# Split weights in three buffers in the input projections, and the odd layer's queries, keys and values in passes over 512 columns

## The chip, the cores and the metric

The kernel runs on one core of a Trainium2 chip. The metric is the device time of one execution in microseconds, the median of several; the profile is one further execution, taken by the hardware profiler.

## What is computed

Two sequences, of 1024 and 2048 tokens with 1024 channels, go through two layers with shared weights. The even layer projects the normed input, feeds half of it to a bidirectional S5 mixer and half to a bidirectional RWKV-7 mixer, gates both and projects back. The odd layer is windowed attention:

```python
def odd_layer(x, p):
    h = rms_norm(x, p['norm'])
    o = attn_branch(h @ p['w_in'], p)
    return x + (o.astype(x.dtype) @ p['w_out']).astype(x.dtype)

q, k, v, z = jnp.split(h, [1024, 1280, 1536], axis=-1)        # of h @ w_in
q = rms_head(q, p['at_q_norm']) * 64 ** -0.5                  # 16 heads of 64
k = rms_head(k, p['at_k_norm'])                               # 4 heads of 64
```

The S5 branch keeps 64 complex states in each of 32 groups of 16 channels and adds a direct term with `s5_d`. The RWKV branch takes r, k and v (512 columns each) and two low-rank inputs (128 columns) from the same projection, shifted by one token to both sides.

## The kernel before

Four programs run one after the other: `input_u` with `s5_consts` (normalize, project u, store the normed tokens h and u), `input_rkv` with `s5` (project r, k, v and the low-rank inputs, beside the S5 mixer), the mixers (gates and RWKV), and `even_out`, `odd_in` and `attention` together. In the first, second and last, class `Program` records every instruction and puts them in an order of its own: `put` (lines 345 to 396) keeps a list for each engine, estimates costs, and sends each engine's instructions in that order. Therefore nearly all instructions carry line 412 in the trace and are told apart by tile and shape. Every tile of a program lies in a few arenas named `sb` and `ps`; a new program takes over the memory of the one before.

All large products are made in two parts: a float32 operand is split into a rounded `hi` and a rest `lo`, and each product is hi·hi + hi·lo + lo·hi, three matmuls per block of 128 rows, 24 per product (`product_T`, line 593; `project_rows`, line 1725).

`input_u` (line 651) stores u in four parts of 128 channels, each 1024 tokens in one store, and then writes zeros into the four columns that separate the two sequences (lines 673 to 677).

`input_rkv` (line 698) goes over six segments of 512 tokens. For each it loads the stored tokens (`stored_T`, eight loads through a tile `full` with three buffers, each split by ACT and DVE) and makes 13 products of 128 columns: the low-rank inputs first (block 12), then for p = 0 to 3 the blocks k, r, v (4+p, p, 8+p). `split_weight` (line 635) loads a block of weights and splits it in the first segment, stores it to `wsp`, and loads it from there, 1 MB, in the others. The tile `wboth` has two buffers (line 723): a weight can be loaded when the product before the last one is done.

`s5` (line 1583) makes 8 rounds of four groups. Each round computes `cw` on DVE (6 operations of 1152 columns), the inverse products `wi0`, `wi1` on DVE (6 operations of 1024 columns), the strip on PE (matmuls with 16 output rows), stores the strip and loads it back twice in another layout as `k0`, and transposes the inverse products on PE into `iw`. Then each group loads its u, makes products with `iw` (`px`) and, after a scan, with `k0` and `cw` (`py`).

`odd_in` (line 1824) goes over the same six segments; per segment it makes 6 passes over 256 columns of the weights for queries, keys and values (two token tiles share one PSUM bank), normalizes by heads on ACT, DVE and POOL (the power on POOL), and then 8 products of 128 columns for the gate z, whose moving operand is 512 tokens.

## Time and profile before

| | us |
|---|---|
| median of 3 runs | 4057.89 (4054.45 to 4062.0) |
| the profiled execution | 4065.39 |
| its span (first to last instruction) | 4063.7 |
| PE busy | 3763.6 (93%) |
| DVE busy | 2821.8 (69%) |
| ACT busy | 1939.8 (48%) |
| POOL busy | 1615.8 (40%) |
| mean granted clock of TensorE | 0.970 |

A busy PE is not a PE at its peak: matmuls overlap, and their ends are modelled. The count of matmuls in a stretch without gaps tells their rhythm better than their mean duration. A wait stands in brackets behind the instruction that ended it, with what released it. SPq is the queue from which all transfers are issued; a DMA share of 1.0 is 16 engines busy.

### The profile page before, as it was taken

Reading aid. Unit: us, or ns where it says so; the run is one execution under the profiler, and the core shown is the slowest. Engines: PE = TensorE matmul, PEld = TensorE weight load, DVE = VectorE, ACT = ScalarE, POOL = GpSimd, SP = SyncE. Lnnn points to the kernel's source line nnn. Section 1 sums busy time; section 2 is a strip of 40 time slices with the busy share of each in tenths; the row PEclk is TensorE's granted clock in tenths of the full one; section 3 lists DMA queues with packets and bytes.
Section 4 is the critical chain, followed back from the end, with each engine's and each line's share of the span. In section 5 each row is a group of like instructions: output and inputs, shape, how many; then the busy total and the mean of one; then the engine's idle time right before and its main releaser. Section 6 shows DMA issues by size and latency. Waiting matters only on the chain.

```text
span 4063.7 us, 87721 instructions
## 1 busy us (share of the span) xinstructions
PE 3763.6 (93%) x34128; PEld 3118.4 (77%) x34128; DVE 2821.8 (69%) x5545; ACT 1939.8 (48%) x4847; POOL 1615.8 (40%) x2007
## 2 busy tenths in 40 slices
PE   6878999999899999999998799999999999999999
PEld 4656766676688888878876577999999977778777
DVE  8356655666568878888887676544444469899997
ACT  3334333333345565555655322333323357777776
POOL 4422322232364555555540242222222335555554
PEclk9989999999999999999999899999999999999999
DMA  5677565566543334333344666644444422222221
GB/s 154 162 174 228 162 191 173 174 191 188 176 154 101 119 112 127 119 106 115 119 115 98 216 233 214 206 148 155 143 157 147 147 84 72 77 81 74 76 66 58
DMA packets 536324, 570.32 MB, mean 140 GB/s; under 512 B 93602, under 2 KB 436770, under 8 KB 525924
## 3 DMA queue, kind: packets, MB, share of 16 engines
q1 hardware_dynamic: 535908, 564.72, 45.4%
q8 instruction: 268, 4.39, 0.5%
q14 instruction: 148, 1.21, 0.1%
HBM read 398.03 MB, written 166.56 MB: 139 GB/s over the span
## 4 chain that ended last, share of the span: by engine, by line
PE 45%; DVE 17%; DMA 4%; issue 4%; POOL 3%; ACT 2%; SPq 1%; DVEq 0%; ACTq 0%; POOLq 0%
PE ps L412 30%; DVE sb L412 11%; PE acc L887 5%; PE pc L1333 2%; PE acc L970 2%; PE pg L1186 2%; ACT sb L412 2%; DMA rk<-rk 1%; DVE ng L1251 1%; DVE z L1253 1%; PE pY L1356 1%; PE pc L1320 1%; POOL lt L1165 1%; PE pc L1311 1%; DVE lt L1206 1%
## 5 line engine op out<-in xcount | busy, mean ns | idle before, releaser
L412 PE MATMUL ps<-sb 128*128 128x512 f32 (+8 forms) x12464 | 2542.2, 359 | 153.2 <-DVE sb L412 48.4
L412 PEld LDWEIGHTS ps<-sb 128*128 128x128 f32 (+2 forms) x12464 | 1958.8, 187 | 555.7 <-DVE sb L412 105.0
L412 POOL TENSOR_TENSOR sb<-sb,sb 128x384 f32<-128x384 f32 (+5 forms) x468 | 469.5, 1021 | 444.2 <-ACT sb L412 226.0
L412 POOL TENSOR_TENSOR sb<-sb 128x512 f32<-128x512 f32 (+5 forms) x358 | 320.7, 899 | 675.0 <-ACT sb L412 325.8
L412 DVE TENSOR_TENSOR sb<-ps,sb 128x512 fp32r<-128x512 f32 (+4 forms) x620 | 402.0, 661 | 189.7 <-PE ps L412 115.5
L412 POOL TENSOR_TENSOR sb<-sb,mhalf 128x8 f32<-128x8 f32 (+3 forms) x156 | 223.0, 1431 | 644.4 <-DVE sb L412 640.5
L887 PE MATMUL acc<-h,w 128*128 128x128 f32 x3072 | 448.0, 290 | 17.0 <-POOL rt L1280 14.3
L887 PEld LDWEIGHTS acc<-h,w 128*128 128x128 f32 x3072 | 383.1, 196 | 42.5 <-POOL rt L1280 14.5
L412 ACT ACTIVATE sb<-sb 128x256 fp32r<-128x256 f32 (+9 forms) x392 | 276.1, 710 | 286.3 <-DVE sb L412 128.5
L412 ACT COPY sb<-ps 128x512 f32<-128x512 f32 (+4 forms) x402 | 195.1, 502 | 438.0 <-PE ps L412 429.3
L412 PE MATMUL ps<-ident,sb 128*128 128x128 f32 x1888 | 317.2, 280 | 55.5 <-DVE sb L412 51.1
L412 DVE TENSOR_TENSOR sb<-sb,sb 128x256 fp32r<-128x256 f32 (+6 forms) x259 | 265.8, 1038 | 142.9 <-ACT sb L412 128.8
L412 ACT ACTIVATE sb<-sb,sb 128x384 f32<-128x384 f32 (+3 forms) x486 | 299.3, 619 | 111.5 <-DVE sb L412 60.4
L412 PEld LDWEIGHTS ps<-ident,sb 128*128 128x128 f32 x1888 | 237.6, 143 | 119.9 <-DVE sb L412 72.1
L1165 POOL TENSOR_TENSOR lt<-rk,lb 64x256 f32<-64x256 f32 x288 | 216.9, 761 | 196.3 <-PE pY L1356 84.8
L412 ACT ACTIVATE sb<-ps 128x512 f32<-128x512 f32 x108 | 64.5, 597 | 385.7 <-PE ps L412 385.7
L1325 ACT COPY rt<-pc 32x128 f32<-32x128 f32 x768 | 196.7, 256 | 97.7 <-PE pc L1320 86.6
L412 DVE CUSTOM_DVE_ANT_0 sb<-ps,sb,sb 128x384 f32<-128x384 f32 (+1 forms) x384 | 215.3, 588 | 28.6 <-PE ps L412 27.1
L1150 POOL TENSOR_TENSOR kb<-rk,f 128x128 f32<-128x128 f32 x384 | 197.6, 546 | 76.1 <-PE pg L1196 67.6
L412 ACT CAST sb<-ps 128x512 fp32r<-128x512 f32 x368 | 202.1, 587 | 50.9 <-PE ps L412 46.0
L1340 DVE TENSOR_TENSOR rt<-pc,wc 64x256 f32<-64x256 f32 x376 | 158.3, 421 | 71.5 <-PE pc L1334 36.1
L412 DVE TENSOR_SCALAR sb<-sb,sb 128x384 f32<-128x384 f32 (+4 forms) x264 | 190.6, 751 | 18.2 <-POOL sb L412 16.2
(121 smaller groups left out, 4680.1 us busy)
## 6 DMA issues: line engine op xcount, KB each, us to landing
sb<-wsp SPq DMA_DIRECT2D x65, 1024.0 KB
rk<-rk SPq DMA_DIRECT2D x96, 512.0 KB
sb<-in_od_w_in SPq DMA_DIRECT2D x36, 1024.0 KB
h<-h SPq DMA_DIRECT2D x48, 512.0 KB
sb<-in_od_w_z SPq DMA_DIRECT2D x24, 1024.0 KB
qkv<-sb SPq DMA_DIRECT2D x72, 256.0 KB
sb<-qkv SPq DMA_DIRECT2D x72, 256.0 KB
sb<-in_x_sample SPq DMA_DIRECT2D x32, 512.0 KB
```

What stands on the lines that cost most here:

```text
L412: self.ops.append((eng, self.cost(eng, op, outs[-1] if outs[-1] is not k.get("accum_out") else outs[0], ins, a, k), deps, self.rank, lambd ...
L887: nc.tensor.matmul(sums[n][1][:, m * P:m * P + P], w[:, k, m * P:m * P + P], acts[n][0][:, k], start=k == 0, stop=k == KT - 1)
L970: nc.tensor.matmul(ps[:, 256 * (m % 2):256 * (m % 2) + 256], uw_at(k)[:, m], act_at(n)[:, 2 * k:2 * k + 2], start=k == 0, stop=k == 3)
L1150: nc.gpsimd.tensor_tensor(kb[:, sl, :, x, :], arr[n][:, sl, cs], f1[:, sl, cs, a:a + 32], MULT)
L1165: (nc.gpsimd if eng == "POOL" else nc.vector).tensor_tensor(ltv[:, :, :, at:at + 32], arr[n][rows, :, cs], f2[rows, :, cs, off:off + 32], ...
L1186: nc.tensor.matmul(g[64:P, c1, p], kb[0:64, p, c1].rearrange("c s i -> c (s i)"), lt[0:64, c1, 4 + p, 0:64], start=True, stop=True)
L1206: nc.vector.tensor_tensor(lt[rows, :, us, 0:64], g[rows], self.tri[h["d"]][rows].unsqueeze(1).unsqueeze(1).broadcast_to([64, 2, 4, 64]), MULT)
L1251: nc.vector.tensor_tensor(tv, z[:, 0:k, k:k + 1].broadcast_to([P, k, 31 - k]), z[:, k:k + 1, k + 1:32].broadcast_to([P, k, 31 - k]), MULT)
L1253: nc.vector.tensor_tensor(z[:, 0:k, k + 1:32], z[:, 0:k, k + 1:32], tv, ADD)
L1325: nc.scalar.copy(rt[rows, c1, 2 * q:2 * q + 2, :], pu[rows, 2:4])
L1333: nc.tensor.matmul(pu[0:64, 4 + p, :], lt[:, c1, 4 + p, 64:P], rt[:, c1, 4 + p, :], start=True, stop=True)
L1340: nc.vector.tensor_tensor(nrt[rows, n4 % 2, 4 - 4 * o:8 - 4 * o, :], pu[rows, 4:8], nh["wc"][rows, :, n4:n4 + 1].broadcast_to([64, 4, 64]) ...
```

## The change

Four parts. `input_u` gives its output tiles four more columns, clears them on POOL for the last part of the first sequence, and stores them with u; the four stores of zeros go. In `input_rkv` the pools are opened first, the pool of the weights has three buffers, and block 12's weight and the tokens of a segment are asked for together by `lead`, for the first segment ahead of the column loads. In `s5` the strip, its store and the loads of `k0` come ahead of the inverse products; the strip and both inverse products share the one buffer of a tile `wi`. In `odd_in` the six passes over 256 columns become three over 512: `wide_weight` loads two halves into tiles of 512 columns with two buffers, one token tile fills one PSUM bank, and the last pass holds the keys (normalized) and the values (copied).

```diff
+    WW = 2
...
+    def wide_weight(self, w):
+        nc = self.nc
+        hi = self.wp.tile([P, KT, 512], F32R, name="whi512", bufs=self.WW)
+        lo = self.wp.tile([P, KT, 512], F32R, name="wlo512", bufs=self.WW)
+        for c in (0, 256):
+            raw = self.wp.tile([P, KT, 256], F32, name="wraw256", bufs=2)
+            nc.sync.dma_start(raw, w[:, c:c + 256].rearrange("(k p) c -> p k c", p=P))
+            nc.scalar.copy(hi[:, :, c:c + 256], raw)
+            nc.vector.tensor_tensor(lo[:, :, c:c + 256], raw, f32(hi[:, :, c:c + 256]), SUB)
+        return [[x[:, k, :] for k in range(KT)] for x in (hi, lo)]
...
-                us = [op.tile([P, 8, min(1024, max(self.L)) // 8], F32, name=f"u{p}")[:, :, :T // 8] for p in range(4)]
+                us = [op.tile([P, 8, min(1024, max(self.L)) // 8 + 4], F32, name=f"u{p}") for p in range(4)]
+                pad = 4 if s == 0 and t0 + T == L else 0
+                if pad:
+                    for x in us:
+                        nc.gpsimd.memset(x[:, :, T // 8:T // 8 + pad], 0.0)
...
-        zero = cp.tile([P, 8, 4], F32, name="zero")
-        nc.gpsimd.memset(zero, 0.0)
-        n0 = self.col[0] + self.L[0] // 8
-        for p in range(4):
-            nc.sync.dma_start(self.u[p].rearrange("g c j n -> (g c) j n")[:, :, n0:n0 + 4], zero)
...
-        self.wp = st.enter_context(tc.tile_pool(name="wp", bufs=2))
+        self.wp = st.enter_context(tc.tile_pool(name="wp", bufs=3))
+        lead = lambda s, t0: (self.split_weight(12, W[:, LW0:LW0 + P]), self.stored_T(self.sp[s]["h"], t0, min(self.seg, self.L[s] - t0)))
+        first = lead(0, 0)
...
-                h = self.stored_T(t["h"], t0, T)
+                (w12, h), first = first or lead(s, t0), None
...
-            wr = [wp.tile(shp, F32, name=f"wi{i}") for i in range(2)]
-            strip = wp.tile([16, NG, 31, 16], F32, name="strip")
+            strip = wp.tile([16, 2 * NG * 256], F32, name="wi")[:, :NG * 496].rearrange("c (g t i) -> c g t i", g=NG, i=16)
...
+            wi = wp.tile([P, 2, NG, 16, 16], F32, name="wi")
+            wr = [wi[:, i] for i in range(2)]
...
-                for c in range(6):
-                    wt = self.weight([W[:, 256 * c:256 * c + 256]])
-                    for i in range(0, nt, 2):
-                        ps = self.psm.tile([P, 2, 256], F32, name="acc")[:, :n]
+                for c in range(3):
+                    wt = self.wide_weight(W[:, 512 * c:512 * c + 512])
+                    for i in range(nt):
+                        ps = self.psm.tile([P, 512], F32, name="acc")
+                        self.project_rows(None, [(his[k][:, sl], los[k][:, sl]) for k in range(8)], wt, slice(0, 512), ps)
+                        n = 512 if c < 2 else 256
+                        if c == 2:
+                            nc.scalar.copy(o[:, n:], ps[:, n:])
...
+                        nc.sync.dma_start(t["qkv"][ti // 2][:, ti % 2, 512 * c:512 * c + 512], o)
```

The order that comes of it differs at three places that the prediction speaks of. The first is SP's queue where the second program begins; `u_0` to `u_3` are the stores of u and of the zeros, `in_rw_...` the column loads, `h0_0` the tokens of the first segment, `in_ev_w_in` a block of weights, `wsp12` the store of block 12. Before:

```order
L412 DMA u_3_228<-sb1_283 1024x1x128
L412 DMA u_2_227<-sb0_282 1024x1x4
L412 DMA u_3_228<-sb0_282 1024x1x4
L412 DMA sb0_1644<-in_rw_mu 128x13x1
L412 DMA sb0_1644<-in_rw_k_k 128x4x1
L412 DMA sb0_1644<-in_rw_k_a 128x4x1
L412 DMA sb0_1644<-in_rw_r_k 128x4x1
L412 DMA sb0_1644<-in_rw_a0 128x4x1
L412 DMA sb1_1645<-in_rw_a_up 64x512
L412 DMA sb1_1645<-h0_0_106 128x4x128 x3
L412 DMA sb1_1645<-in_ev_w_in 128x8x128
L412 DMA sb1_1645<-u_0_225 128x1x388 x2
```

With the change:

```order
L412 DMA u_3_228<-sb1_283 1024x1x128
L412 DMA sb1_1644<-in_ev_w_in 128x8x128
L412 DMA sb1_1644<-h0_0_106 128x4x128 x3
L412 DMA sb0_1643<-in_rw_mu 128x13x1
L412 DMA sb0_1643<-in_rw_k_k 128x4x1
L412 DMA sb0_1643<-in_rw_k_a 128x4x1
L412 DMA sb0_1643<-in_rw_r_k 128x4x1
L412 DMA sb0_1643<-in_rw_a0 128x4x1
L412 DMA sb1_1644<-in_rw_a_up 64x512
L412 DMA sb1_1644<-u_0_225 128x1x388 x2
L412 DMA wsp12_253<-sb2_1645 128x2048
L412 DMA sb1_1644<-h0_0_106 128x4x128 x3
```

The stores of 4 columns are gone, the weight and three token loads stand first, and the store of the split weight stands ahead of the next token loads.

The second is SP's queue at the fourth of the eight strips; `wsp9`, `wsp6` and `wsp2` are weights in the order in which PE uses them, `strip3` is the strip's store and its two loads. Before:

```order
L412 DMA bon1_144<-sb1_1645 64x384 x2
L412 DMA rk1_126<-sb1_1645 128x3x128
L412 DMA sb2_1646<-wsp9_250 128x2048
L412 DMA strip3_236<-sb1_1645 16x1984
L412 DMA sb1_1645<-strip3_236 128x4x256 x2
L412 DMA sb2_1646<-wsp6_247 128x2048
L412 DMA rk1_126<-sb1_1645 128x3x128 x2
L412 DMA sb2_1646<-wsp2_243 128x2048
L412 DMA rk1_126<-sb1_1645 128x3x128
```

With the change:

```order
L412 DMA bon1_144<-sb1_1644 64x384 x2
L412 DMA rk1_126<-sb1_1644 128x3x128
L412 DMA sb2_1645<-wsp6_247 128x2048
L412 DMA strip3_236<-sb1_1644 16x1984
L412 DMA sb1_1644<-strip3_236 128x4x256 x2
L412 DMA sb2_1645<-wsp2_243 128x2048
L412 DMA sb2_1645<-wsp10_251 128x2048
L412 DMA rk1_126<-sb1_1644 128x3x128 x2
L412 DMA bon1_144<-sb1_1644 64x384 x2
```

Weight 6 stood behind the strip's loads and stands ahead of the strip's store now; weight 2 is the first one behind them.

The third is PE at the same strip: the last strip products (16 rows) and what follows; `ps0` and `ps1` with 128x512 are the projections, `ps4` with 128x128 the transposes of the inverse products. Before:

```order
L412 MATMUL ps4_1654<-sb1_1645 16x256 x2
L412 MATMUL ps4_1654<-sb1_1645 16x16 x2
L412 MATMUL ps4_1654<-sb1_1645 16x240 x2
L412 MATMUL ps1_1651<-sb2_1646 128x512 x5
L412 MATMUL ps4_1654<-ident_60,sb1_1645 128x128 x4
L412 MATMUL ps1_1651<-sb2_1646 128x512
L412 MATMUL ps2_1652<-heads2_67,sb1_1645 128x2 x3
L412 MATMUL ps1_1651<-sb2_1646 128x512 x2
L412 MATMUL ps4_1654<-ident_60,sb1_1645 128x128
L412 MATMUL ps1_1651<-sb2_1646 128x512
L412 MATMUL ps4_1654<-ident_60,sb1_1645 128x128
```

With the change:

```order
L412 MATMUL ps4_1653<-sb1_1644 16x240
L412 MATMUL ps0_1649<-sb2_1645 128x512
L412 MATMUL ps4_1653<-sb1_1644 16x240
L412 MATMUL ps3_1652<-sb1_1644 128x384
L412 MATMUL ps1_1650<-sb2_1645 128x512 x14
L412 MATMUL ps2_1651<-heads2_67,sb1_1644 128x2 x3
L412 MATMUL ps1_1650<-sb2_1645 128x512 x10
L412 MATMUL ps0_1649<-sb2_1645 128x512 x4
L412 MATMUL ps3_1652<-ident_60,sb1_1644 128x128 x3
L412 MATMUL ps0_1649<-sb2_1645 128x512 x4
L412 MATMUL ps4_1653<-ident_60,sb1_1644 128x128 x2
L412 MATMUL ps0_1649<-sb2_1645 128x512 x16
```

Before, five projection matmuls stood between the last strip product and the transposes; now there are 32.

## Rows read from the trace of the kernel before

**Rows 1.** The page: busy time by engine, and the chain that ended last.
```profile
PE 3763.6 (93%) x34128; PEld 3118.4 (77%) x34128; DVE 2821.8 (69%) x5545; ACT 1939.8 (48%) x4847; POOL 1615.8 (40%) x2007
...
PE 45%; DVE 17%; DMA 4%; issue 4%; POOL 3%; ACT 2%; SPq 1%; DVEq 0%; ACTq 0%; POOLq 0%
```

**Rows 2.** Stretches: second program, attention; length, busy (count) by engine, clock, DMA share, GB/s.
```profile
246.00:1100.00 854.00, 787.01 (x3662) 592.73 (x3662) 533.16 (x762) 316.19 (x696) 245.58 (x245) 0.96 0.63 188
...
3500.00:3600.00 100.00, 95.74 (x564) 78.50 (x562) 91.82 (x246) 77.95 (x217) 59.12 (x78) 1.00 0.26 83
```

**Rows 3.** The same view of the odd projections: one narrow stretch, one wide (gates).
```profile
2590.00:2650.00 60.00, 60.00 (x503) 60.00 (x502) 33.75 (x50) 22.39 (x29) 30.67 (x24) 1.00 0.54 181
2660.00:2690.00 30.00, 30.00 (x134) 24.82 (x134) 9.97 (x8) 8.40 (x8) 0.00 (x0) 1.00 0.42 146
```

**Rows 4.** Groups by shape, 2590 to 3280 us: busy us, mean ns, idle before.
```profile
L412 ACT ACTIVATE sb<-sb 128x2048 fp32r<-128x2048 f32 x58 | 110.7, 1909 | 0.0
L412 POOL TENSOR_TENSOR sb<-sb,mhalf 128x8 f32<-128x8 f32 x60 | 102.9, 1714 | 148.2 <-DVE sb L412 148.2
```

**Rows 5.** Timeline where the second program begins: start, duration, instruction, [wait before it].
```profile
234.58 2.61 POOL L412 MEMSET sb<- 128x392 f32 x13 [25.50 <-DMA u<-sb]
234.59 2.63 DVE L412 TENSOR_TENSOR sb<-pw,cc 128x1152 f32<-128x1152 f32 x2 [26.89 <-DMA u<-sb]
```

**Rows 6.** Stretches of the last u stores: length, clock, DMA share, GB/s.
```profile
214.00:224.00 10.00, 0.99 1.01 179
224.00:226.00 2.00, 0.50 1.54 55
...
229.00:232.00 3.00, 0.50 1.19 64
```

**Rows 7.** Timeline up to the second program's first product.
```profile
234.48 0.38 SPq L412 DMA_DIRECT2D sb<-in_rw_mu  x1
...
237.86 1.69 SPq L412 DMA_DIRECT2D sb<-h  x3
...
239.59 0.51 SPq L412 DMA_DIRECT2D sb<-in_ev_w_in  x1
...
245.04 1.04 ACT L412 CAST sb<-sb 128x1024 fp32r<-128x1024 f32 x1 [1.40 <-DMA sb<-in_ev_w_in]
...
246.13 10.15 PE L412 MATMUL ps<-sb 128*128 128x512 f32 x40 [5.61 <-ACT sb L412]
```

**Rows 8.** PE's waits from 246 to 1100 us: total us, times, longest.
```profile
PE ps L412 <- DVE sb L412: 23.3, 20, 3.6
PE ps L412 <- DMA sb<-wsp: 23.2, 10, 4.9
PE ps L412 <- ACT sb L412: 18.1, 10, 5.6
PE ps L412 <- DMA sb<-strip: 7.5, 2, 5.8
```

**Rows 9.** Timeline of PE: first and last of the four longest waits for stored weights.
```profile
611.60 5.08 PE L412 MATMUL ps<-sb 128*128 128x512 f32 x12 [4.70 <-DMA sb<-wsp]
...
934.87 6.11 PE L412 MATMUL ps<-sb 128*128 128x512 f32 x14 [4.45 <-DMA sb<-wsp]
```

**Rows 10.** Timeline of SP at the fourth strip.
```profile
592.92 0.32 SPq L412 DMA_DIRECT2D strip<-sb  x1
595.44 1.30 SPq L412 DMA_DIRECT2D sb<-strip  x2
599.70 0.33 SPq L412 DMA_DIRECT2D sb<-wsp  x1
```

**Rows 11.** Lower clock behind the first and last of these: length, PE busy (count), clock, DMA.
```profile
609.50:616.30 6.80, 4.70 (x12) 0.50 0.57 213
...
933.80:940.50 6.70, 5.63 (x13) 0.50 0.36 143
```

**Rows 12.** Timeline of DVE: one of the inverse products.
```profile
601.53 1.23 DVE L412 TENSOR_TENSOR sb<-ip,bb 128x1024 f32<-128x1024 f32 x1 [1.51 <-PE ps L412]
```

More of the change, by code (lines that the diff above doesn't have):

```diff
@@ L1640, in s5 @@
                 nc.scalar.copy(strip[:, g].rearrange("q t c -> q (t c)"), pk[0:16, 0:496])
-            for g in range(NG):
-                pt = ps.tile([P, 512], F32, name="pk")
-                for i in range(2):
-                    for h in range(2):
-                        nc.tensor.transpose(pt[:, (2 * i + h) * P:(2 * i + h + 1) * P], wr[i][:, g, 8 * h:8 * h + 8].rearrange("q j c -> q (j c)"), self.ident)
-                nc.scalar.copy(iw[:, g].rearrange("q i h c -> q (i h c)"), pt)
             dd = wp.tile([16, NG, 16], F32, name="dd")
```

80 lines of the change are left out of this document (40 added, 40 removed).

## The prediction

> **What bounds the kernel now.** I read the page first for the engines and the chain, then the trace cut into stretches, then the waits of single stretches. The page gives PE 93% of the span and the largest share of the chain that ended last [rows 1], so PE is the engine to follow; but the average hides three regimes. From about 246 to 1100 us runs the second program (the projections for r, k, v beside the S5 mixer): PE is busy 787 of 854 us at a mean clock of 0.96, so some 67 us of it are waits of PE [rows 2]. In the odd layer's projections PE is busy in every microsecond at full clock (60 of 60, 30 of 30), while DVE is busy for 34 of 60 us and 10 of 30 [rows 3]. In the attention behind it DVE is at 92% and the change touches nothing [rows 2]. So in the odd projections only the work of PE itself can be made shorter; in the second program only what PE waits for.
>
> **The change, part by part.** The sum is made against the profiled execution, 4065.4 us (span 4063.7), which stands 7.5 us above the median of the three runs, 4057.9; I subtract the same sum from that median.
>
> *The odd layer's passes.* Six segments of 512 tokens, 6 passes, 4 token tiles, 24 matmuls each are 3456 matmuls over 256 columns; the change makes 1728 over 512 of them. A mean duration in a list is no price here, since matmuls overlap; I take the rhythm of stretches where PE runs without a gap. 503 narrow ones in 60 us, two of which only reach into the window, give 60/501 = 119.8 ns; 134 wide ones in 30 us, counted alike, give 30/132 = 227.3 ns [rows 3]. A pair of narrow ones against one wide one saves 239.5 - 227.3 = 12 ns; with the counts as printed 2 x 119.3 - 223.9 = 14.7 ns. I take 13 ns: 1728 x 13 = **22.5 us**, bounds 20.7 and 25.4, all of it on the path, as PE has no gap there. The wide stretch is one of the gate projections; nothing in it moves less data per matmul. The loads stay at 36 of 1 MB, now two per pass; the splits on ACT and DVE stay in number and size (on ACT 58 of 1.9 us in this stretch) and lie beside PE [rows 4]. The normalization goes from 10 sets of eight heads and two copies per segment to 8 sets of eight, 4 of four heads and 4 half copies: POOL's power, 1.7 us each, was called 10 times and is now called 12 times a segment, on an engine half idle [rows 3, 4]. I cost these at nothing; if the cover were gone, two more powers would be 3.4 us per segment. The first pass of a segment now needs two loads before its first matmul; in the order both stand among the gate stores of the segment before, and the gate projections cover them with 192 matmuls x 227 ns = 44 us.
>
> *The zero columns.* The second program's first instructions all waited until the last store of u had landed, DVE for 26.9 us, and that wait ended at 234.5 [rows 5]. Four of the last stores are the zero pads, 16 KB each in runs of 16 bytes. In the two stretches where the transfers crawl (55 and 64 GB/s with the engines fully occupied) five microseconds moved 2 x 55 + 3 x 64 = 302 KB; at the 179 GB/s of the stretch before that takes 1.7 us [rows 6]. The pads now ride as 16 more bytes on runs of 512 written much earlier: **3.3 us** gained, bounds 2 and 5. The four added clears on POOL, 32 columns each, come at the start of the program, before its first product is copied; thirteen clears of up to 392 columns take 2.6 us together [rows 5], so they cost nothing that counts.
>
> *The first loads moved up.* Before, six column loads and three token loads stood ahead of the first weight: issue at 239.59, landed for ACT at 245.04, first product at 246.13 after 5.6 us of waiting for ACT alone [rows 7]. Now the weight is the first issue, 239.59 - 234.48 = 5.1 us earlier. What follows pays some of it back: the store of the split weight, which waits for DVE behind four products of 1.3 us each, now stands ahead of token loads four to six on SP, and the six columns (3.4 us of issue) ahead of both; nothing waits for the columns before the first product is done. Bounds 0 and 5.1; I take **3 us**, nearer the upper end because PE's wait of 5.6 us names the weight, not the tokens.
>
> *Three buffers and the S5 order.* Of the 67 us PE waited 23.2 for stored split weights, 7.5 for the S5 strips, 23.3 for DVE and 18.1 for ACT [rows 8]. Four waits, of which the first took 4.70 us and the last 4.45, make most of it, some 18 of the 23.2 [rows 9], and each follows a strip; at the first of them the strip is stored at 592.92, two loads of it go out at 595.44, the next weight waits for its buffer until 599.70, queues behind the strip's loads and reaches PE at 611.60, 18.7 us after the store was issued [rows 9, 10]. Two things change. With three buffers the weight that came behind the strip's loads now stands ahead of the store. And the inverse products come behind the strip, so PE's order puts the transposes later: between the last strip product and the first product whose weight stands behind the strip's loads the order has 47 wide matmuls at the fourth strip before, and 72 now (34 to 51 over the eight strips before, 48 to 79 now, 63 or more from the second on). 47 x 0.227 = 10.7 us, with some 3.5 us of small matmuls, ends before the 18.7 us; 72 x 0.227 = 16.3 us with the same small ones ends behind them. So those waits should go. I take 20 of the 23.2 us (bounds 0 and 23.2), and 5 of the 7.5 for the strips, since the strip's loads no longer come last in the S5 chain (bounds 0 and 7.5). Behind each of the four waits the clock stood at its lower level (0.50, that is 1.2 GHz): PE worked 4.70 us there at the first and 5.63 at the last, 20 us at all four, and at full clock that is 10 us [rows 11]. I take 8 (bounds 0 and 10). New waits come in exchange: DVE cannot start the inverse products before the strip is stored, because both now share one tile; 2.5 us from store to release [rows 10] and five products of 1.2 us [rows 12] are 8.6 us, of which the order covers 26 to 41 wide matmuls, 5.9 to 9.3 us. I charge 5 us for the eight strips together (bounds 0 and 16). Balance **28 us** gained; the 41 us for DVE and ACT I leave as they are.
>
> **Sum:** 22.5 + 3.3 + 3 + 28 = 56.8 us. 4065.4 - 56.8 = 4008.6 for a profiled execution; from the median 4057.9 - 56.8 = **4001 us**.
>
> The Trainium skill, "TensorE: Matmul & The Clock Gate", section "Back-to-back issue gap", puts the slot of a warm matmul at its columns over 2.4 GHz plus 2.5 ns, 262 cycles for 256 columns and 518 for 512. By it the merged passes would save 6 cycles a pair, an estimate of 4.3 us instead of 22.5. The trace disagrees on both sizes, 119.8 and 227.3 ns against 109 and 216 [rows 3].
>
> **The rivals.**
> - *The waits move.* The second program keeps its length because DVE (busy 533 of 854 us) and ACT become what PE waits for as soon as the weights are early. For it: PE already waits 41 us for them, in 30 pieces. Against it: DVE is at 62% there [rows 2]. Then only 22.5 + 3.3 + 3 = 28.8 us remain: 4029. The same time comes out if the third buffer does not bring the loads forward because the queue in front of them is still blocked.
> - *The wide pass saves little.* If what a narrow pass loses lies in the columns and not in each matmul (the rule that stands in the section named above), the passes give 4.3 us: 4001 + 18.2 = 4019. Against it stand the counts of two stretches without a gap [rows 3].
> - *Slower.* The shared tile puts store and inverse products in a row at each of eight strips, and PE stands before the transposes. The price is the 8.6 us if PE has nothing else ready: 8 x 8.6 = 69 us, less 28.8: 4098. It decides from 28.8/8 = 3.6 us of wait per strip on, with the weight waits gone for nothing. Against it: the order puts 5.9 us or more of ready products there.
> - *More.* All waits for weights and strips go and no new ones come: 40.7 instead of 28, and with the upper bounds of the others 3982 or a little under.
>
> **How the numbers follow.** The forecast (3982 to 4020) has 0.68, the moved waits 0.17, the wide pass that saves little 0.04, slower 0.06, more than the forecast 0.05. The range takes in the forecast and the moved waits with a few microseconds of spread (the runs before lie 7.6 us apart): 3974 to 4036, which leaves out the slower case and what lies beyond the upper bounds. A measurement of this kernel tells about 0.2%, 8 us, from no change; of the moved waits 0.04 may end there. Faster 0.68 + 0.13 + 0.04 + 0.05 = 0.90, same 0.04, slower 0.06.
>
> **What would show it.** In the new profile the odd projections should hold no narrow stretch, 132 wide matmuls per 30 us throughout, and end some 22 us closer to their start. The second program should begin about 3 us sooner after the last u store was issued, PE's first product within 7 us of it. PE's waits for stored weights should fall from 23.2 to a few us, the lower clock level should be rarer in that stretch, and PE should reach the transposes without more than 1 to 2 us of wait at a strip. I am wrong if the wide matmuls take 230 ns or more, if PE's total wait in the second program stays above 60 us with DVE or ACT as the name, or if a new gap opens where the odd projections begin or end.

## The result, and the profile after

| us | before | with the change |
|---|---|---|
| median | 4057.73 (4 runs, 4054.45 to 4062.0) | **4016.94** (4 runs, 4012.84 to 4020.61) |
| ratio, 95% interval | | 0.9897 [0.9883, 0.9911] |
| the profiled execution | 4065.39 | 4020.61 |
| its span | 4063.7 | 4018.9 |

The kernel became 40.8 us faster (36 to 47 by the interval). The forecast was 4001, its range 3974 to 4036. The sum was 16 us too large by the medians, 12 by the two profiled executions, and this hides more than it shows: one term was 6.5 us too small, another 20.6 us too large.

The page of the kernel after, beside [rows 1]:

```profile
PE 3736.1 (93%) x32400; PEld 3024.2 (75%) x32400; DVE 2833.3 (70%) x5581; ACT 1941.7 (48%) x4871; POOL 1632.1 (41%) x2034
PE 50%; DVE 14%; DMA 3%; issue 3%; POOL 3%; ACT 2%; SPq 1%; DVEq 0%; POOLq 0%; ACTq 0%
```

PE lost 1728 matmuls, as it should; its share is the same 93%. Where the 44.8 us between the two profiled executions lie is read by cutting both traces at the same places of the program:

| stretch | before | after | gain | predicted |
|---|---|---|---|---|
| up to the landing of the last u store | 234.5 | 229.5 | 5.0 | 3.3 |
| from there to the end of the second program | 865.5 | 855.1 | 10.4 | 3 + 28 |
| odd projections | 706.2 | 677.2 | 29.0 | 22.5 |
| mixers, even_out, attention together | | | 0.4 | 0 |

The stretch of the second program before and after (length, busy time and count of PE, PEld, DVE, ACT, POOL, then granted clock, DMA share, GB/s):

```profile
234.50:1100.00 865.50, 788.02 (x3664) 592.87 (x3664) 543.75 (x776) 320.41 (x704) 248.80 (x261) 0.95 0.63 187
```

```profile
229.50:1084.60 855.10, 783.10 (x3664) 589.24 (x3664) 552.23 (x776) 320.25 (x704) 260.00 (x261) 0.96 0.64 190
```

PE stood idle for 77.5 us before and for 72.0 now. Of its busy time 62.3 us fell into stretches at the lower clock level before (each busy interval laid over the records of the granted clock), and 51.6 now; counted half, the work at full clock is 756.9 and 757.3 us, the same. So the 10.4 us are 5.5 us of idle time and 10.7/2 = 5.3 us of clock, and nothing else.

PE's waits after, from 241 to 1105 us (total us, times, longest), beside [rows 8]:

```profile
PE ps L412 <- DVE sb L412: 26.2, 25, 3.6
PE ps L412 <- ACT sb L412: 18.9, 13, 5.4
PE ps L412 <- DMA sb<-strip: 17.6, 6, 4.6
...
PE ps L412 <- DMA sb<-u: 2.7, 1, 2.7
```

The 23.2 us for stored weights are gone entirely. In their place PE waits 10.1 us longer for the strip, 2.7 for u, 2.9 for DVE and 0.8 for ACT.

One of the new waits, at the sixth strip; first SP's queue, then PE:

```profile
790.09 1.31 SPq L412 DMA_DIRECT2D sb<-strip  x2
```

```profile
797.58 0.59 PE L412 MATMUL ps<-sb 128*128 128x196 f32 x2 [0.72 <-DMA sb<-strip]
802.78 1.02 PE L412 MATMUL ps<-sb 128*128 128x196 f32 x2 [4.61 <-DMA sb<-strip]
```

The loads went out at 790.09, and PE could use the second of them at 802.78, 12.7 us later. The planner sets 1.46 us for each load (512 KB at 360 GB/s) and 2 us of latency, 5 us for the two together. (The price stands in `cost`, at line 358 of the kernel before; `put`, which orders by it, starts at line 414 and not at 345.) Three of the eight strips have such waits, the first, second and sixth: PE came to their products 4.5, 5.9 and 6.8 us behind the issue. In the kernel before, at the same strip, SP and then PE:

```profile
814.88 1.46 SPq L412 DMA_DIRECT2D sb<-strip  x2
```

```profile
825.99 3.07 PE L412 MATMUL ps<-sb 128*128 128x196 f32 x12 [1.69 <-DMA sb<-strip]
```

There PE had 9.4 us of other products behind the issue, and waited 1.69 us. One other strip made PE wait in the kernel before; its products came 7.9 us behind the issue.

### The profile page after: what moved, and what is told of

Same layout as the page of the kernel before. It is cut to its first block, busy times and chain, and to the rows that moved or that the text cites. A ratio compares the mean times of both kernels' runs of the same rounds, so it can differ in the third digit from the quotient of the medians.

```text
span 4018.9 us, 84393 instructions
## 1 busy us (share of the span) xinstructions
PE 3736.1 (93%) x32400; PEld 3024.2 (75%) x32400; DVE 2833.3 (70%) x5581; ACT 1941.7 (48%) x4871; POOL 1632.1 (41%) x2034
## 4 chain that ended last, share of the span: by engine, by line
PE 50%; DVE 14%; DMA 3%; issue 3%; POOL 3%; ACT 2%; SPq 1%; DVEq 0%; POOLq 0%; ACTq 0%
PE ps L412 32%; DVE sb L412 10%; PE acc L905 6%; PE pc L1351 2%; PE pg L1204 2%; PE acc L988 2%; PE pY L1374 1%; PE pc L1338 1%; PE pc L1329 1%; POOL lt L1183 1%; DMA rk<-rk 1%; ACT sb L412 1%; PE pg L1214 1%; DMA sb<-bon 1%; POOL kb L1168 1%
## 5 line engine op out<-in xcount | busy, mean ns | idle before, releaser
L412 PE MATMUL ps<-sb 128*128 128x512 f32 (+5 forms) x10736 | 2503.6, 386 | 137.7 <-DVE sb L412 49.7
L412 PEld LDWEIGHTS ps<-sb 128*128 128x128 f32 (+1 forms) x10736 | 1857.5, 185 | 601.4 <-DVE sb L412 111.4
L412 POOL TENSOR_TENSOR sb<-sb,sb 128x512 fp32r<-128x512 f32 (+5 forms) x480 | 461.7, 980 | 381.0 <-DVE sb L412 206.9
L412 POOL TENSOR_TENSOR sb<-sb 128x512 f32<-128x512 f32 (+5 forms) x358 | 337.0, 945 | 637.6 <-DVE sb L412 283.2
L412 DVE TENSOR_TENSOR sb<-ps,sb 128x512 fp32r<-128x512 f32 (+5 forms) x632 | 403.8, 652 | 171.9 <-PE ps L412 94.5
L412 POOL TENSOR_TENSOR sb<-sb,mhalf 128x8 f32<-128x8 f32 (+4 forms) x168 | 224.9, 1340 | 671.9 <-DVE sb L412 663.3
L412 ACT COPY sb<-ps 128x512 f32<-128x512 f32 (+5 forms) x414 | 196.4, 492 | 470.4 <-PE ps L412 445.7
L412 PE MATMUL ps<-ident,sb 128*128 128x128 f32 x1888 | 314.1, 280 | 52.6 <-DVE sb L412 50.6
L412 ACT ACTIVATE sb<-sb,sb 128x384 f32<-128x384 f32 (+3 forms) x486 | 299.3, 619 | 126.3 <-DVE sb L412 60.5
L412 DVE TENSOR_TENSOR sb<-sb,sb 128x256 fp32r<-128x256 f32 (+6 forms) x259 | 264.8, 1037 | 116.3 <-ACT sb L412 97.0
L412 ACT ACTIVATE sb<-sb 128x256 fp32r<-128x256 f32 (+7 forms) x356 | 208.0, 589 | 281.2 <-DVE sb L412 124.4
L412 PEld LDWEIGHTS ps<-ident,sb 128*128 128x128 f32 x1888 | 239.2, 144 | 120.5 <-DVE sb L412 69.0
L412 ACT CAST sb<-sb 128x512 fp32r<-128x512 f32 (+4 forms) x289 | 202.0, 714 | 166.1 <-DMA sb<-in_od_w_in 43.7
L412 DVE CUSTOM_DVE_ANT_0 sb<-ps,sb,sb 128x384 f32<-128x384 f32 (+1 forms) x384 | 215.3, 587 | 28.7 <-PE ps L412 26.7
L412 ACT CAST sb<-ps 128x512 fp32r<-128x512 f32 x368 | 202.1, 587 | 50.1 <-PE ps L412 46.2
L412 DVE TENSOR_SCALAR sb<-sb,sb 128x384 f32<-128x384 f32 (+4 forms) x264 | 190.7, 751 | 15.3 <-POOL sb L412 13.3
```

Source lines behind the costliest of these rows:

```text
L412: self.ops.append((eng, self.cost(eng, op, outs[-1] if outs[-1] is not k.get("accum_out") else outs[0], ins, a, k), deps, self.rank, lambd ...
```

## The experiments

All ratios are to the kernel before, run beside them on the same chip; the changed kernel stands at 0.9897. The runs come from several chips, so a few microseconds between two of them mean nothing.

### The odd passes alone

The kernel before with `wide_weight` and the three passes over 512 columns, as in the diff of the change; nothing else.

> The kernel before with the odd layer's wide passes alone; everything else as it was. Theory A (the odd passes gave 28 us, because a wide matmul saves 13 ns a pair and the small waits at the start of each segment shrink as well): the odd projections end 28 us sooner after their start, the time is 4057.7 - 28.4 = 4029 us, ratio 0.993; the second program keeps its waits of 23 us for stored weights. Rival (the passes gave the 22.5 us of the prediction and some 6 us came from other parts of the change that reach into the odd layer): 4035 us, ratio 0.9945.

Measured 4039.18 us, ratio 0.995 [0.9936, 0.9965]. The odd projections before, with the change, and in this run (the same columns as above):

```profile
2582.80:3289.00 706.20, 700.31 (x4795) 650.70 (x4793) 314.77 (x392) 236.94 (x289) 182.07 (x151) 1.00 0.46 151
```

```profile
2567.20:3244.40 677.20, 674.56 (x3066) 557.57 (x3064) 317.38 (x427) 234.97 (x311) 181.82 (x175) 1.00 0.47 157
```

```profile
2587.30:3264.80 677.50, 673.99 (x3062) 557.33 (x3061) 317.42 (x427) 236.46 (x312) 182.36 (x175) 1.00 0.47 157
```

The passes alone shorten the odd projections by 28.7 us, all of what the whole change gives there. The total fell by only 20 us (14 to 26), less than theory A's 28.4. The stage speaks for theory A, the total for the rival's number. What lies between them sits in no single stage: between the profiled executions the second program, whose code is untouched, is 2.4 us longer (11.9 us of waits for the strip where the profile of before has 7.5), the programs from there to the odd projections 2.1 us and the attention 2.0 us. The cause of these 6.5 us is open. In what follows the waits and stages of the traces are therefore read beside the ratios.

### Two buffers again

```diff
-        self.wp = st.enter_context(tc.tile_pool(name="wp", bufs=3))
+        self.wp = st.enter_context(tc.tile_pool(name="wp", bufs=2))
```

> The changed kernel with two buffers for the split weights again; the new order of the S5 round, the moved loads, the merged zeros and the wide passes stay. Theory A (the third buffer is what took the waits for stored weights away): they come back with 10 us or more, the second program gets 10 us longer than in the changed kernel, 4027 us. Rival (the new order of the S5 round took them away, by putting more products between a strip and the weight behind it): waits for stored weights stay under 5 us, 4017 us within 4.

Measured 4061.6 us, ratio 1.0003 [0.999, 1.0015]: the whole gain is lost, 43 us by the ratios, four times what I expected. PE's waits from 241 to 1090 us:

```profile
PE ps L412 <- DMA sb<-strip: 36.2, 11, 6.3
PE ps L412 <- DVE sb L412: 26.3, 23, 2.5
PE ps L412 <- ACT sb L412: 11.2, 7, 5.1
PE ps L412 <- DMA sb<-wsp: 11.1, 10, 4.6
```

The waits for stored weights come back with 11.1 us, as theory A said, but the larger part is the strip, 36.2 us. (The second program ends at 1123.4 here; behind 1090 there is one more wait, 3.6 us for DVE.) From the landing of the last u store (230.6) to its end it took 892.8 us, 38 us more than with the change and 27 us more than before it. The moved round on two buffers is a loss; the third buffer carries it.

### The strip behind the inverse products

With three buffers and a tile of its own for the strip, the old round needs 190.3 KB per partition where 183.7 are left, so it does not fit and has no time. This kernel keeps the shared tile and exchanges the two halves of the round:

```diff
+            shp = [P, NG, 16, 16]
+            wi = wp.tile([P, 2, NG, 16, 16], F32, name="wi")
...
             strip = wp.tile([16, 2 * NG * 256], F32, name="wi")[:, :NG * 496].rearrange("c (g t i) -> c g t i", g=NG, i=16)
...
-            shp = [P, NG, 16, 16]
-            wi = wp.tile([P, 2, NG, 16, 16], F32, name="wi")
```

> The changed kernel with the two halves of the S5 round exchanged back: inverse products and their transposes first, then the strip in the same shared tile, its store and its loads. Three buffers, moved loads, merged zeros and wide passes stay. Theory A (the strip first is what puts the products with it close behind the loads; with the transposes first PE has the products with the inverse to do meanwhile): PE's waits for the strip fall under 9 us, waits for stored weights stay under 5, 4005 to 4012 us. Rival (the shared tile now holds the strip up until the transposes are done, and the loads stand ahead of the weights again): waits for stored weights or the strip of over 20 us, 4025 us or more.

Measured 4058.85 us, ratio 0.9984 [0.9971, 0.9997]. PE's waits, the same stretch:

```profile
PE ps L412 <- DMA sb<-strip: 48.0, 14, 6.2
PE ps L412 <- DVE sb L412: 20.3, 26, 2.1
PE ps L412 <- ACT sb L412: 12.7, 6, 7.1
PE ps L412 <- DMA sb<-u: 3.3, 1, 3.3
```

My theory A falls: with the strip last PE waits 48 us for it, not under 9. In this form the strip's place at the front is not what makes PE wait; but the shared tile stays, and whether it is the tile that brings the products so close behind the loads no run separates. Of the weights it shows the other half: with three buffers there is no wait for a stored weight in either order of the round. Without the third buffer 11.1 us of them remain, so the buffer is needed. What the order gives isn't separated, since in both runs PE waits 36 or 48 us for the strip, and weights can land meanwhile.

### A higher price for the strip's loads in the planner

```diff
-        return math.prod(out.shape) * 4 / 360e3
+        slow = ins[0].space == DRAM and out.space != DRAM and ins[0].tensor.shape[-1] == 16 and len(ins[0].ap) == 4 and ins[0].ap[0][0] == 16
+        return math.prod(out.shape) * 4 / (90e3 if slow else 360e3)
```

> The changed kernel; only the cost that the planner puts in for the two loads that bring the strip back is four times as high (5.8 us each instead of 1.46), so that it puts the products with the strip later; the transfers themselves stay as they are. Theory A (the order puts these products too close behind the loads, because their cost is set too low): PE's waits for the strip fall from 17.6 us to under 6 and the time falls by 10 to 15 us, to 4002 to 4007 us from a level of 4017. Rival (the loads also hold up everything behind them on the queues, which no order hides): the waits move to DVE, ACT or the stored weights, and the time stays within 5 us of 4017.

Measured 4008.89 us, ratio 0.9866 [0.9851, 0.9881]. The line of the strip among PE's waits:

```profile
PE ps L413 <- DMA sb<-strip: 12.5, 4, 4.3
```

(L413 is L412 of the others, one line further down.) The ratio falls by 0.31%, some 12 us, as theory A said, and the second program takes 842.8 us instead of 855.1; but the waits for the strip fall only from 17.6 to 12.5 us, not under 6. A better price helps; it does not hide the loads.

### What makes the strip's loads slow: four corners

The source of a load is a pattern of 8 token offsets (step 16 numbers) by 16 channels (step 1984) by 4 groups, in runs of 256 numbers. Three kernels with the order of every engine unchanged vary the pattern (the two with overlapping rows read wrong numbers, so they are measurements and no versions of the kernel):

```diff
-bass.AP(tensor=x.tensor, offset=x.offset + 16 * (8 - 8 * h), ap=[[16, 8], [NG * 496, 16], [496, NG], [1, 256]])
+bass.AP(tensor=x.tensor, offset=x.offset + 128 * h, ap=[[240, 128], [1, 1024]])
...
+bass.AP(tensor=x.tensor, offset=x.offset + NG * 16 * (8 - 8 * h), ap=[[NG * 16, 8], [NG * 496, 16], [1, 1024]])
...
+bass.AP(tensor=x.tensor, offset=x.offset + 128 * h, ap=[[232, 128], [496, NG], [1, 256]])
```

The second of them stores the strip as (row, column, group), so that a row's four groups lie together, and takes `k0[:, i, P * e:P * e + P, g]` as weights.

> The changed kernel, the order of every engine unchanged, but the two loads that bring the strip back read the same number of bytes from the same tensor in runs of 4 KB (overlapping rows) instead of 1 KB; the direct term of the S5 branch is therefore not computed from the right numbers. Theory A (the loads of the strip take 7 to 13 us because of their 1 KB runs, the order allows some 5): the landing comes within 6 us of the issue, PE's waits for the strip fall from 17.6 us to under 5, the second program gets 10 to 15 us shorter: 4003 to 4007 us. Rival (other transfers ahead in the queues, not the runs, set the landing): it stays above 7 us, PE's waits for the strip above 10 us, time within 5 us of 4017.

> The changed kernel with the strip stored as (row, column, group) instead of (row, group, column), so that the two loads that bring it back read 1024 consecutive numbers (4 KB) for each row instead of four times 256; the products with it take weights of 128 columns at a stride of four numbers. The result is the reference's, and the order of every engine stays. Theory A (the 1 KB runs are what makes these loads slow, and nothing else in the run with the overlapping rows was gained by reading other numbers): the time comes within 5 us of 3995 us, PE's waits for the strip stay under 5 us. Rival (the overlapping rows were faster because they are near each other in memory, or weights at a stride load slower, 128 products of 196 columns): PE's waits for the strip stay above 10 us or the products with the strip take over 0.6 us each, 4010 us or more.

> The changed kernel, the order of every engine unchanged; the two loads that bring the strip back keep their runs of 1 KB but read 128 rows at one even step (overlapping) instead of 8 rows of 16, so the direct term of the S5 branch is not computed from the right numbers. With the run of 4 KB rows at an even step (3995 us) and the run of 4 KB rows in 8 times 16 (4022 us) this is the fourth corner. Theory B (8 as the first count of the source's pattern keeps the load on 8 of the 16 DMA engines; the Trainium skill says so of a first count under 16 in DMA: Bandwidth & Descriptors, Rules for kernel authors): the loads land within 8 us, PE's waits for the strip fall from 17.6 us to under 5, and the time is 0.5% or more under the changed kernel, ratio to the kernel before 0.983 to 0.986. Rival (only long runs and an even step together help; 1 KB runs stay slow): waits for the strip above 10 us, ratio 0.988 or more.

| source pattern | runs | ratio | us from first issue to the last packet's end, mean of 8 strips | PE's waits for the strip |
|---|---|---|---|---|
| 8 x 16 rows (the changed kernel) | 1 KB | 0.9897 | 12.3 | 17.6 |
| 8 x 16 rows | 4 KB | 0.9894 [0.9878, 0.9911] | 12.0 | 17.0 |
| 128 rows at an even step | 4 KB | 0.9842 [0.9825, 0.9858] | 5.5 | none |
| 128 rows at an even step | 1 KB | 0.9828 [0.9801, 0.9855] | 5.4 | 0.6 |

The landing times are worked out from the records of the packets, which have a size of their own in these loads. The run length decides next to nothing, so theory A of the first two runs was wrong in its reason: the run over 4 KB rows became faster for how its rows are counted. With the fast loads the second program takes 827.0 and 827.8 us instead of 855.1, so what these two ratios gain on the changed kernel, some 22 and 28 us, lies there. PE's waits for the strip, with 8 x 16 rows in runs of 4 KB and with 128 rows in runs of 1 KB:

```profile
PE ps L412 <- DMA sb<-strip: 17.0, 6, 4.7
```

```profile
PE ps L412 <- DMA sb<-strip: 0.6, 1, 0.6
```

Two stretches show the difference while the loads of a strip are under way, first with the change (issued at 692.82), then with 128 rows of 1 KB (issued at 684.32):

```profile
698.00:702.00 4.00, 4.00 (x19) 3.24 (x18) 4.00 (x6) 0.89 (x2) 1.17 (x1) 1.00 1.08 176
```

```profile
685.00:689.00 4.00, 4.00 (x20) 3.24 (x19) 4.00 (x5) 1.62 (x3) 1.64 (x1) 1.00 0.96 297
```

At about the same share of the DMA engines the one moves 176 GB/s, the other 297. The Trainium skill, "DMA: Bandwidth & Descriptors", sections "Why a DMA increments its semaphore by 16 and not by 1" and "Rules for kernel authors", says that the largest number up to 16 that divides the slowest count of both patterns is the number of engines used, so a first count of 8 would keep a load on 8 of 16. The four corners agree with it, 12.3 against 5.4 us. The trace names no engine for a packet, but it records the semaphore that counts a load's landing. In each of the 16 loads of the changed kernel one update came early (1.06 us behind the issue in one of them) and eight at the landing (6.8 to 7.1 us); with 128 rows none came early and sixteen at the landing (3.2 to 3.5 us), in all 11 loads beside which nothing else counts on the same semaphore. Eight and sixteen are the numbers that the rule gives. The packets of 1 KB themselves took 87 ns each in the changed kernel and 54 in the last run, which the rule alone doesn't say.

### The same in the kernel before

The same layout (runs of 4 KB, still 8 x 16 rows) in the kernel before.

> The kernel before with the same layout of the strip (runs of 4 KB), nothing of the change. Theory A (the loads of the strip are also what held the stored weights up in the kernel before): PE's waits for stored weights fall from 23.2 us to under 8 and those for the strip from 7.5 to under 2, with half of the 10 us of lower clock: the time falls by 25 to 30 us, ratio 0.993 to 0.994. Rival (the weights came late because with two buffers they cannot be asked for earlier): waits for stored weights stay above 15 us, and the time falls by under 12 us.

Measured 4067.41 us, ratio 1.0016 [1.0003, 1.0029]: waits for stored weights 20.9 us, for the strip 9.2. As the layout does not make the loads faster, this run says nothing on whether slow strip loads held the weights up. What it does show is a price: PE's work at full clock is 769.6 us in the second program instead of 757, and 770.2 in the changed kernel with this layout. Weights read at a step of four numbers cost PE some 13 us.

### Sixteen rows first, with the right numbers

Rows ordered by channel and then token in u, in the inverse products and in the reloaded strip, so that 16 is the first count; the inverse products are made in halves and written at a step of 8:

```diff
-            self.cmul(wr[0], wr[1], ir, ii, br, bi, t1)
+            for h in range(2):
+                ir, ii = (x[:, gs, 8 * h:8 * h + 8].unsqueeze(3).broadcast_to(shp) for x in self.ip)
+                self.cmul(*(w[:, :, h].rearrange("q g c j -> q g j c") for w in wr), ir, ii, br, bi, t1)
...
+bass.AP(tensor=x.tensor, offset=x.offset + NG * 16 * (8 - 8 * h), ap=[[NG * 496, 16], [NG * 16, 8], [1, 1024]])
```

> The changed kernel with the strip as (row, column, group) and the rows of u, of the inverse products and of the reloaded strip ordered by channel and then token instead of token and then channel. The loads of u and of the strip then read 16 times 8 rows instead of 8 times 16, and the strip's still 4 KB runs. The result is the reference's. The inverse products are made in 12 operations of 512 columns instead of 6 of 1024, so the planner's order is another one. Theory B (a first count of 16 puts the loads on all 16 DMA engines): the strip lands within 7 us of the issue, PE's waits for it are under 5 us, and the time is 3995 us within 8, less some 5 us for the loads of u and plus some 5 us for weights read at a stride: ratio 0.981 to 0.986. Rival (the even step, not the count of engines, made the loads fast): waits for the strip above 10 us, ratio 0.988 or more.

> The run before it (rows ordered by channel, the strip by row, column, group), and the planner's cost of these loads is twice as high, since they land about 5 us after the issue where the planner expects some 3.5 for the first. Theory B: it gives a few us more if waits for the strip or u are left, ratio 0.980 to 0.985; PE's waits for strip and u together under 3 us. Rival (the planner's cost was only wrong because of the slow loads): no difference to the run before it within 5 us.

Measured 4022.04 us, ratio 0.990 [0.988, 0.9919], and with the higher price 4016.7, 0.9881 [0.9863, 0.99]. PE's waits of the first, from 241 to 1090 us:

```profile
PE ps L412 <- DVE sb L412: 44.5, 48, 4.7
PE ps L412 <- ACT sb L412: 9.6, 8, 4.3
PE ps L412 <- DMA sb<-strip: 0.7, 2, 0.5
```

The strip lands 6.7 us after the issue and PE no longer waits for it, as theory B said. These loads read the same rows as the 8 x 16 rows in runs of 4 KB, in another order (16 x 8), and land in 6.7 us instead of 12.0, with sixteen updates of the semaphore at the landing: it is the first count, and an even step is not needed. The forecast of the time fails all the same. DVE's products with the inverse, in the changed kernel and here, from 300 to 1000 us:

```profile
L412 DVE TENSOR_TENSOR sb<-ip,bb 128x1024 f32<-128x1024 f32 x25 | 32.1, 1298 | 2.9 <-DMA strip<-sb 2.9
```

```profile
L412 DVE TENSOR_TENSOR sb<-ip,bb 128x512 f32<-128x512 f32 x49 | 45.2, 968 | 2.4 <-DMA strip<-sb 2.3
```

Half an operation takes 968 ns, not half of 1298, and PE waits 18 us longer for DVE; weights at a step take their share again (773.8 us of work at full clock). The 968 ns are a mean of two kinds with the same patterns of input: the 25 whose output lies in a row in a scratch tile have a median of 694 ns, the 24 that write at a step of 8 one of 1160. So it is the step in what DVE writes. (The 1024 columns in a row have a median of 1211 to 1223 ns.) With the higher price no wait for the strip or u is left, as expected, but the time misses its forecast too and differs from the first by less than the intervals.

### Eight loads of sixteen rows: the version that beats both

```diff
-            for h in range(2):
-                nc.sync.dma_start(k0[:, h], bass.AP(tensor=x.tensor, offset=x.offset + 16 * (8 - 8 * h), ap=[[16, 8], [NG * 496, 16], [496, NG], [1, 256]]))
+            for a in range(8):
+                nc.sync.dma_start(k0[16 * a:16 * a + 16], bass.AP(tensor=x.tensor, offset=x.offset + 16 * a, ap=[[NG * 496, 16], [496, NG], [128, 2], [1, 256]]))
...
-                        nc.tensor.matmul(py[:, e], k0[:, i, g, P * e:P * e + P], uh[i], start=i == 0, stop=False)
+                        nc.tensor.matmul(py[:, e], k0[:, g, 1 - i, P * e:P * e + P], uh[i], start=i == 0, stop=False)
```

> The changed kernel with the strip brought back by eight loads of 16 rows (one for each token of eight, both halves in one load, runs of 1 KB as before) instead of two loads of 8 times 16 rows; the result is the reference's, the weights read without a stride, the inverse products as in the changed kernel. Theory B (a first count of 16 rows puts a load on all 16 DMA engines): although SP issues eight loads instead of two (some 3 us instead of 1.3), the last lands within 9 us of the first issue instead of 12.3; PE's waits for the strip fall from 17.6 us to under 6, and DVE's work does not grow, so ratio to the kernel before 0.983 to 0.987 (the changed kernel 0.990). Rival (eight issues in a row on SP hold the weights and tokens behind them up, or the new order of the planner costs what the loads give): ratio 0.988 or more, with waits for stored weights or ACT 5 us above the changed kernel's.

Measured **4003.13 us, ratio 0.9847 [0.982, 0.9873]** (5 runs): 0.5% under the changed kernel, their intervals apart. SP at a strip, and PE's waits from 241 to 1090 us:

```profile
677.04 0.32 SPq L412 DMA_DIRECT2D strip<-sb  x1
679.57 5.56 SPq L412 DMA_DIRECT2D sb<-strip  x8
685.23 2.01 SPq L412 DMA_DIRECT2D sb<-wsp  x2
```

```profile
PE ps L412 <- DVE sb L412: 29.7, 29, 4.8
...
PE ps L412 <- ACT sb L412: 10.9, 7, 5.1
PE ps L412 <- DMA sb<-strip: 10.1, 3, 5.6
PE ps L412 <- DMA sb<-u: 1.3, 1, 1.3
```

The ratio is the one expected; two of its steps are not. The eight issues take 5.6 us instead of 3, the last packet ends 9.7 us after the first issue instead of under 9, and 10.1 us of waits for the strip are left instead of under 6. Most of the 9.7 us is the issue: the last of the eight loads goes out 5.3 us after the first (mean of the eight strips), and its last packet ends 4.4 us later. The loads gain 2.6 us of the 6.9 that 128 rows gain, with slower packets (109 ns in place of 87); why these are slower is open. PE's idle time in the second program falls from 72.0 to 58.2 us, and its work at the lower clock from 51.6 to 37.5.

### The first loads not moved up

```diff
-        first = lead(0, 0)
+        first = None
```

> The changed kernel with the weight and the tokens of the first segment asked for behind the column loads again; the rest stays. Theory A (the first loads moved up brought PE's first product 6 us nearer to the last store of u, but PE waits 4.9 us for tokens 14 us later, so little of it is kept): the first product starts about 5 us later and the time rises by 0 to 3 us, ratio to the kernel before 0.989 to 0.991. Rival (most of what the second program gained, 10 us, came from these loads): the time rises by 6 us or more, ratio 0.9915 or more.

Measured 4019.29 us, ratio 0.9893 [0.9872, 0.9914]: no difference to the changed kernel. PE at the start of the second program, with the change and in this run:

```profile
235.45 5.33 PE L412 MATMUL ps<-sb 128*128 128x512 f32 x11 [15.71 <-ACT sb L412]
241.27 1.52 PE L412 MATMUL ps<-sb 128*16 128x256 f32 x10 [0.49 <-DVE sb L412]
247.64 14.47 PE L412 MATMUL ps<-sb 128*128 128x512 f32 x49 [4.85 <-ACT sb L412]
```

```profile
236.67 1.01 PE L412 MATMUL ps<-sb 128*16 128x256 f32 x2 [15.98 <-DMA sb<-in_rw_a_up]
241.41 7.75 PE L412 MATMUL ps<-sb 128*128 128x512 f32 x31 [3.73 <-ACT sb L412]
249.81 12.46 PE L412 MATMUL ps<-sb 128*16 128x256 f32 x56 [0.65 <-ACT sb L412]
```

With the moved loads the first product starts at 235.45 instead of 241.41, or, counted from the last landing of u, 5.9 us behind it instead of 9.7. But after 11 matmuls PE waits 4.85 us for tokens: ACT, which ends this wait, had itself waited 9.6 us for their load. The second line's ten small products stand ahead of the tokens with the change, and behind 31 wide matmuls without.

## Why the prediction was right in its sign and wrong in its parts

**What bounds the kernel.** Right. PE has the same work in the second program before and after, 757 us at full clock; only what it waits for and its clock changed. (The four groups of waits before, 72.1 us, hold 5.6 us that lie ahead of 246, so they are not parts of the prediction's 67.) In the odd projections it was PE's own work, but for 3.3 us.

**The odd passes, 22.5 us: 29.0.** The mechanism was right and the size too small. PE's busy time there fell by 700.3 - 674.6 = 25.7 us, 14.9 ns for each of 1728 pairs. That is the counts as printed (14.7) and not my compromise of 13; my upper bound of 25.4 was 0.3 us short. Another 3.3 us are idle time, 5.9 before and 2.6 now, which I had costed at nothing. It lies where a segment begins; PE before, at one of the five starts that have such waits, and after:

```profile
2697.74 0.50 PE L412 MATMUL ps<-sb 128*128 128x256 f32 x2 [0.39 <-ACT sb L412]
2698.54 0.66 PE L412 MATMUL ps<-ident,sb 128*128 128x128 f32 x4 [0.31 <-DVE sb L412]
...
2704.34 1.10 PE L412 MATMUL ps<-sb 128*128 128x256 f32 x7 [0.34 <-DVE sb L412]
```

```profile
2790.83 1.20 PE L412 MATMUL ps<-sb 128*128 128x512 f32 x4 [0.39 <-ACT sb L412]
```

Three waits of 0.3 to 0.4 us became one. A wide product between two transposes gives ACT and DVE twice the time, which is how I read it; no run tests it. The windows with their wide matmuls stood as forecast, with no gap:

```profile
2700.00:2730.00 30.00, 30.00 (x134) 24.83 (x133) 17.61 (x20) 10.44 (x10) 15.49 (x12) 1.00 0.64 211
```

By the formula that the Trainium skill, "TensorE: Matmul & The Clock Gate", section "Back-to-back issue gap", gives, the passes would have saved an estimated 4.3 us; the page gives it for a single matmul by itself, which the prediction left out. For this stream of matmuls it is no price: with the passes alone PE's busy time fell by 700.3 - 674.0 = 26.3 us.

**The zero columns, 3.3 us: 5.0.** Right in sign, at its upper bound in these two traces: the stores of u were done at 229.5 instead of 234.5. In the other runs they were done between 228.4 and 232.1 with the merged zeros, and at 234.5 and 237.8 without, so the size is known to a few microseconds only, 2.4 us at the least; no run changes the zeros alone.

**The first loads, 3 us: nothing that can be measured.** PE's first product came 10.7 us earlier (246.13 to 235.45), 5.0 us of it from the zero columns; the other 5.7 are more than I had forecast, and the run without the moved loads is as fast. The step that failed is "nearer the upper end because PE's wait of 5.6 us names the weight, not the tokens". The tokens were next: what I wrote down as paid back, token loads behind the store of the split weight, paid back all, as far as the intervals can tell.

**The second program, 28 us: 10.4, with the moved loads' 3 in it.** This is where the forecast went wrong. That 4016.9 still lies in the range is in part luck: the terms that were too small made up for 8 of the 20.6 us that were missing here. Term by term:
- *Stored weights, 20 of 23.2.* Right: all 23.2 are gone. Of the two reasons that I gave, the buffer is shown to be needed: with two buffers and the new order 11.1 us remain, with three buffers none remain in either order of the round. That the order's 72 products instead of 47 helped is not shown.
- *The strip, 5 of 7.5 gained.* Wrong in sign: 10.1 us lost. "The strip's loads no longer come last in the S5 chain" was true of the program text, and I took it for the order in time. I had the duration of these loads in hand (they made weights land 18.7 us after a strip's store) and did not ask what the planner believes of them: at three of eight strips it places the products 4.5 to 6.8 us behind loads of 12 us. The bounds of 0 and 7.5 excluded a loss without a reason. That the loads' duration is what PE waits for is shown: with loads of 5.4 us in the same order 0.6 us of the 17.6 remain. Why the new round brings the products closer behind the loads than the old one, whose planner had the same price, is open.
- *Clock, 8 of 10.* 5.3: the waits for weights took their slow stretches along, and the new waits brought others, with 14.5 us of PE's work at the lower clock around those for the strip and 6.5 at the one for tokens.
- *New waits, 5 us for the shared tile.* About right. PE's waits for DVE ahead of transposes rose from 3.9 to 7.5 us, as the groups of all transposes from 246 to 1090 us show, before and after:

```profile
L412 PE MATMUL ps<-ident,sb 128*128 128x128 f32 x315 | 58.8, 279 | 7.7 <-DVE sb L412 3.9 <-ACT sb L412 3.6
```

```profile
L412 PE MATMUL ps<-ident,sb 128*128 128x128 f32 x320 | 58.6, 287 | 8.8 <-DVE sb L412 7.5 <-ACT sb L412 1.1
```

The rival that the waits move came out for the second program, though not by its mechanism alone: DVE and ACT took 3.7 us of the 23.2, the strip's transfer 10.1. My own sign of error, a total wait above 60 us there, came true in its number, 65.4 against 72.1 of the four groups before, though only 45.1 of it names DVE or ACT, 3.7 more than before. The slower rival's mechanism (store and inverse products in a row on a shared tile) cost at most 3.6 us ahead of the transposes and not 69; but what the moved round costs without the third buffer, a second program 27 us longer than before, is close to a change that loses everything, and I had looked for it in the wrong place.

## What to carry to other kernels

When a wait for one transfer goes, look at every transfer that the order places by an estimate, and compare the estimate with a landing in the trace: here 5 us were planned for loads that take 12, and at three of eight strips the difference was the next wait. When a transfer is slow, vary one thing in its pattern at a time, its runs and its first count; the runs looked guilty and were not. And count PE's work at full clock in a stretch before judging a change there: it was 754 to 759 us in every variant that reads its weights in a row, so that idle time and clock were the whole account, and where it was not (770 to 776), a hidden price had come in.

## What was not expected of the hardware

- Two loads of 512 KB landed 12.3 us after their issue when the source began with a count of 8, and 5.4 when it began with 128 rows at an even step, with as many bytes and the same runs of 1 KB. Runs of 4 KB changed neither number by more than 0.3 us. The same rows in runs of 4 KB took 12.0 us counted 8 x 16 and 6.7 counted 16 x 8. The semaphore was counted up eight times at the landing with a first count of 8, and sixteen times with one of 16 or 128.
- Weights read at a step of four numbers cost 13 us of PE's work over the second program (757 to 770).
- DVE took 1160 ns for 512 columns written at a step of 8 and 694 ns for 512 in a row (medians).
- A wide matmul in place of two narrow ones saved 14.9 ns of busy time, over 1728 pairs.
